# Part of a sparse expert layer moved from row gathers to dense products

## The chip, the cores and the metric

One core of a Trainium2 chip runs the whole program. The metric is the device time of one execution in microseconds. A core has a tensor engine (PE), a vector engine (VectorE, DVE), an activation engine (ScalarE, ACT), GpSimd (POOL) and a queue engine (SyncE, SP). Data come from HBM through 16 DMA engines. GpSimd issues the gathers, SP the plain loads, and both kinds share these engines.

## The reference

The program is one transformer layer on 256 latent tokens of width 2048: attention and a gated delta rule side by side, then an expert layer, then a final norm. The change touches the expert layer alone. Each token picks 16 of 16,384 experts for each of 8 heads, through two lists of 128 keys; an expert's number is `128 * i + j`, so there are 128 blocks of 128 experts. Each expert has one row of `u` and one row of `v`, 2048 floats each (8 KiB).

```python
q = (hx @ w_q).reshape(t, 8, 2, 128)
s = jnp.einsum('thpd,pkd->thpk', q, sub_keys)
top_s, top_i = lax.top_k(s, 16)
cand = top_s[:, :, 0, :, None] + top_s[:, :, 1, None, :]
cand_idx = top_i[:, :, 0, :, None] * 128 + top_i[:, :, 1, None, :]
best_s, best_pos = lax.top_k(cand.reshape(t, 8, -1), 16)
idx = jnp.take_along_axis(cand_idx.reshape(t, 8, -1), best_pos, axis=-1)
wts = jax.nn.softmax(best_s, axis=-1)
act = jax.nn.gelu(jnp.einsum('td,thkd->thk', hx, u[idx]), approximate=False)
return jnp.einsum('thk,thkd->td', wts * act, v[idx])
```

## The kernel before

The 256 tokens are two tiles `t` of 128, and the 8 heads two halves `f`. The layer ahead of the experts leaves its input in `hx`, channels on partitions. What follows has five stages.

Queries: for each head two tiles of `w_q` (1 MiB each, loaded by SP into row buffers) meet `hx` in 32 products of 256 columns (`query`), and two small products give the scores (`scores`). `route` turns the scores of a head and a token tile into 16 expert numbers and weights, wholly on VectorE, in small pieces (`piece`) between other work. The u rows of tile 0, half 0 are gathered meanwhile.

Rounds 0 to 2 (`rounds`, `n`): the round of tile and half `(t, f)` has 16 steps `b`. In each step `first` is called four times for the round after: it gathers 128 u rows, one per token (1 MiB), and VectorE multiplies them by the tokens' inputs `h_` and sums (a `SCALAR_TENSOR_TENSOR` of 128 x 2048). Then `second` gathers four times 128 v rows, and PE adds them up with weights in `zw`: 16 products of 32 weight columns by 512, four PSUM tiles `y`, four column groups of 32. `weigh`, at a round's start, applies gelu and the softmax weights and spreads the result into `zw`. Round 3 has v gathers alone.

Products and transposes of PE go through a helper at lines 192 and 197 and all work of DVE through one at line 181, so the profile gives these lines for them; gathers are line 1279. PE and DVE keep the order in which the program is written, and each engine waits in its own order: an instruction that waits holds what is queued behind it. The row buffers of `first`, `second` and the loads of `w_q` are one ring of 13 (`ROWS_R`, `ROWS_L`); an issue waits until the reader of its buffer is done. Besides, a gather's completion is signalled on one of eight semaphores in turn (`DMASW0` to `DMASW7`), and an issue waits for the gather eight before it.

`h_` is a PSUM tile of four banks that PE transposes fill (`hx_tokens`). `finish` adds the result of a token tile to `x1s` and applies the last norm, with two row buffers of its own; for tile 0 it runs in round 2.

Of the kernel before, what the change touches and what calls it, by code (L numbers as in the profile page):

```python
# [26 lines left out]
NEG = -1.0e30  # L27

# [83 lines left out]
def layout(x, c, ctx, c_ctx, w_mod, b_mod, norm1_w, w_in, mla_q_norm_w, mla_kv_norm_w, w_uq, w_ukv, dn_conv_w,  # L112
# [49 lines left out]
    a["u"] = np.ascontiguousarray(peer_u[0])  # L162
    a["v"] = np.ascontiguousarray(peer_v[0])
# [5 lines left out]
def tile_block(ctx: ExitStack, tc: tile.TileContext, I, out, dbg=None, upto=99):  # L169
# [1006 lines left out]
    hx = hxp.tile([128, KB, T], F32, name="hx")  # L1176
# [59 lines left out]
    ROWS_R, ROWS_L = 4, 9  # L1236
    rows = {"n": 0}

    def row():
        i = rows["n"] % (ROWS_R + ROWS_L)  # L1240
        rows["n"] += 1
        p, n = (rp, ROWS_R) if i < ROWS_R else (ex, ROWS_L)
        return p.tile([128, D], F32, name="row", bufs=n)

    def wq_load(i):
        r = row()
        sp.dma_start(r, I["wq"][i])
        return r

    ahead = [wq_load(i) for i in range(4)]  # L1250
# [11 lines left out]
    psa, st_psa = open_pool("psa", space=bass.MemoryType.PSUM)  # L1262
    psb, st_psb = open_pool("psb", space=bass.MemoryType.PSUM)

    def psm(tag):
        return psb.tile([128, 512], F32, name="ps_" + tag, tag=tag, bufs=2)

    def hx_tokens(t):

        o = psa.tile([128, D], F32, name="ps_h", tag="a", bufs=1)  # L1270
        for k in range(KB):
            pe.transpose(o[:, k * 128:(k + 1) * 128], hx[:, k, t * 128:(t + 1) * 128], ident)
        return o

    ex, st_ex = open_pool("ex", side=L)
# [7 lines left out]
    loaded = {"n": 8}  # L1283
    ahead += [wq_load(i) for i in range(4, 8)]
# [13 lines left out]
    for t in range(2):  # L1298
        per.append({n: ex.tile([128, 128], dt, name="%s%d" % (n, t)) for n, dt in
                    (("bs", F32), ("ef", F32), ("ix", U32), ("ixT", U32), ("a", F32))})  # L1300

    def scores(h, q, t, p):
# [3 lines left out]
        if t == 0 and h < 4:  # L1306
            s = ex.tile([128, T], F32, name="s", bufs=2)
        else:
            s = sc[:, h - 4 if t == 0 else 4 + h]
# [3 lines left out]
    def route(t, h, s):  # L1313
# [3 lines left out]
        sml = ex.tile([128, 208], F32, name="sml", bufs=2)  # L1317
# [6 lines left out]
        ij = sml[:, 176:208]  # L1324
# [33 lines left out]
        dve.tensor_reduce(ij, eq3, axis=AX.X, op=OP.add)  # L1358
        dve.scalar_tensor_tensor(ef[:, hs], ij[:, 0:16], 128.0, ij[:, 16:32], op0=OP.mult, op1=OP.add)
# [30 lines left out]
    def first(t, c, h_):  # L1390

        r = gather("u", per[t]["ix"][:, c:c + 1])
        dve.scalar_tensor_tensor(r, r, 1.0, h_, op0=OP.mult, op1=OP.mult, accum_out=per[t]["a"][:, c:c + 1])

    def weigh(t, f):
# [4 lines left out]
        dve.tensor_tensor(a, a, bs, op=OP.mult)  # L1400
        by_choice(lambda u, p, g: zw[f][p, g, 16 * u:16 * u + 496:33], a)

    def second(t, f, b, y):
# [3 lines left out]
        for c in range(4):  # L1407
            cs = slice(c * 512, (c + 1) * 512)
            for g in range(4):
                pe.matmul(y[c][32 * g:32 * g + 32, :], zw[f][:, g, 32 * b:32 * b + 32], rows[g][:, cs],  # L1410
                          start=f == 0 and b == 0, stop=f == 1 and b == 15)

    def finish(t, y):
# [5 lines left out]
        if t == 0:  # L1419
            for i, c in enumerate(cs):  # L1420
                dve.tensor_tensor(tmp[:, c], y[i], g2r[:, c], op=OP.mult)
            yield
        for i, c in enumerate(cs):
            if t == 1:
                dve.tensor_tensor(tmp[:, c], y[i], g2r[:, c], op=OP.mult)
            dve.tensor_tensor(x[:, c], x[:, c], tmp[:, c], op=OP.add)
# [21 lines left out]
    def piece():  # L1448

        while work:  # L1450
            if next(work[0], work) is not work:
                return
            work.pop(0)
# [8 lines left out]
    def query(h, parts):  # L1462

        ws = [ahead.pop(0) for _ in range(2)]
        os_ = [psm("mm") for _ in range(2)]
        q = [ex.tile([128, T], F32, name="q", bufs=4) for _ in range(2)]
        p = psm("g")
        for a, z in parts:
            for j in range(2):
                for k in range(KB):  # L1470
                    pe.matmul(os_[j][:, a:z], ws[j][:, k * 128:(k + 1) * 128], hx[:, k, a:z],
                              start=k == 0, stop=k == KB - 1)
                act.copy(q[j][:, a:z], os_[j][:, a:z])
# [12 lines left out]
    S = {}  # L1486
# [3 lines left out]
    for h in range(1, NH):  # L1490
        all_of(query(h, ((0, 256),)))
        if h < 5:
            work.append(route(0, h, S[h, 0]))
            for c in range(h * 16 - 16, h * 16):
                first(0, c, h_)
                if c % 16 > 2:
                    piece()
                if c % 8 == 7:
                    ahead.append(wq_load(loaded["n"]))
                    loaded["n"] += 1  # L1500
            while work:
                piece()
    for dst, src in ((g2r, modc[:, 80:96]), (fwr, cols[:, C_FN:C_FN + 16])):
        for i in range(0, 16, 4):
            p = psm("g")
            for j in range(4):
                pe.transpose(p[:, j * 128:(j + 1) * 128], src[:, i + j:i + j + 1].to_broadcast([128, 128]), ident)
            act.copy(dst[:, i * 128:(i + 4) * 128], p)
# [55 lines left out]
```

## Time and profile before

| what | value |
|---|---|
| time, median of 3 runs | 2511.69 us (2511.13 to 2518.51) |
| time of the profiled execution | 2511.01 us |
| its span | 2509.2 us |
| PE, DVE, ACT, POOL busy | 1766.9, 1582.4, 700.8, 897.6 us |
| mean DMA rate over the span | 318 GB/s |
| moved by gathers and other GpSimd DMAs | 541.44 MB |
| moved by SP's loads and stores | 246.39 MB |

Busy times of different engines overlap; their sum says nothing. The span is what the profiler saw, and the time is 1.8 us longer than it. Times inside the span count from its start.

### The profile page before, as it was taken

How to read it: one execution, taken by the hardware profiler on the slowest of the kernel's cores; microseconds unless marked ns; L12 is line 12 of the kernel's file. 1: busy time of each engine (PE TensorE's matmuls, PEld its weight loads, DVE VectorE, ACT ScalarE, POOL GpSimd, SP SyncE). 2: the span in 40 equal slices, each digit the busy share in tenths (PEclk: the TensorE clock that was granted, in tenths of full speed). 3: DMA queues.
4: the chain of work that ended last, by engine and by line, in shares of the span. 5: the costliest groups of instructions: out<-in, count | busy, mean ns of one | idle time of the engine just before them, and what ended most of it. 6: DMA issues, size and time to landing. Idle time of an engine off the chain costs nothing.

```text
span 2509.2 us, 28451 instructions
## 1 busy us (share of the span) xinstructions
PE 1766.9 (70%) x9988; PEld 1113.4 (44%) x9988; DVE 1582.4 (63%) x2773; ACT 700.8 (28%) x1636; POOL 897.6 (36%) x1108
## 2 busy tenths in 40 slices
PE   6999889988989999898953545454454544554665
PEld 2578778877878877898843100010000000000111
DVE  5358877778776588885899776656664454444001
ACT  4358556566655543354000100000000010000000
POOL 0000776738476000211333333333333333333331
PEclk8999999999999999999976776777666766667898
DMA  9955433555466587896999999999999989999997
GB/s 327 322 186 168 151 123 102 157 160 169 146 199 201 185 292 251 277 324 227 413 426 421 426 427 427 427 427 426 427 427 427 427 340 426 427 427 426 427 426 309
DMA packets 167375, 796.86 MB, mean 318 GB/s; under 512 B 26273, under 2 KB 45729, under 8 KB 99137
## 3 DMA queue, kind: packets, MB, share of 16 engines
q0 software_dynamic: 75296, 541.44, 51.5%
q1 hardware_dynamic: 76848, 246.39, 29.2%
q10 hardware_dynamic: 15088, 7.22, 1.0%
q8 instruction: 78, 1.28, 0.2%
q14 instruction: 65, 0.52, 0.1%
HBM read 784.75 MB, written 10.23 MB: 317 GB/s over the span
## 4 chain that ended last, share of the span: by engine, by line
DMA 53%; PE 20%; DVE 8%; issue 7%; POOL 6%; ACT 4%; SPq 0%; POOLq 0%; DVEq 0%; ACTq 0%
DMA row<-in_v,ixT 40%; PE ps_mm L192 13%; PE ps_d L192 4%; DMA row<-in_u,ix 4%; DMA raw<-in_wmod 3%; POOL qs L835 3%; POOL tq L833 3%; DMA raw<-in_wout 2%; DVE lo L181 2%; PE ps_r L192 2%; DMA mraw<-in_wmod 1%; DVE row L181 1%; POOL row L1279 1%; ACT hi L259 1%; PE ps_o L192 1%
## 5 line engine op out<-in xcount | busy, mean ns | idle before, releaser
L192 PE MATMUL ps_y<-row,zw 128*32 128x512 f32 x2048 | 573.3, 772 | 521.5 <-DMA row<-in_v,ixT 496.1
L181 DVE SCALAR_TENSOR_TENSOR row<-row,ps_h 128x2048 f32<-128x2048 f32 x256 | 582.1, 2281 | 409.5 <-DMA row<-in_u,ix 398.0
L192 PEld LDWEIGHTS ps_y<-row,zw 128*32 128x32 f32 x2048 | 97.8, 132 | 995.8 <-DMA row<-in_v,ixT 788.3
L1279 POOL DMA_INDIRECT row<-in_v,ixT x256 | 242.9, 949 | 405.4 <-DMA row<-in_v,ixT 302.9
L1279 POOL DMA_INDIRECT row<-in_u,ix x256 | 239.9, 937 | 408.3 <-DMA row<-in_u,ix 242.3
L181 DVE TENSOR_TENSOR lo<-raw,hi 128x512 fp32r<-128x512 f32 x408 | 307.3, 769 | 73.4 <-ACT hi L259 70.3
L192 PE MATMUL ps_mm<-h_hi,hi 128*128 128x256 f32 (+1 forms) x1040 | 341.0, 328 | 10.7 <-DVE gst L181 10.7
L192 PE MATMUL ps_mm<-h_hi,lo 128*128 128x256 f32 (+1 forms) x1040 | 323.4, 311 | 13.3 <-DVE lo L181 13.2
L192 PE MATMUL ps_mm<-h_lo,hi 128*128 128x256 f32 (+1 forms) x1040 | 322.9, 310 | 0.0
L259 ACT CAST hi<-raw 128x512 fp32r<-128x512 f32 x408 | 245.1, 619 | 184.7 <-PE ps_mm L192 123.0
L192 PEld LDWEIGHTS ps_mm<-h_hi,hi 128*128 128x128 f32 x1040 | 203.4, 196 | 31.3 <-DVE gst L181 11.7
L192 PEld LDWEIGHTS ps_mm<-h_hi,lo 128*128 128x128 f32 x1040 | 203.0, 195 | 24.0 <-DVE lo L181 14.5
L192 PEld LDWEIGHTS ps_mm<-h_lo,hi 128*128 128x128 f32 x1040 | 203.4, 196 | 9.3 <-issue 1.2
L835 POOL TENSOR_TENSOR qs<-qs,tq 32x30 f32<-32x30 f32 (+14 forms) x240 | 175.4, 731 | 18.7
L833 POOL TENSOR_TENSOR tq<-qs 32x30 f32<-32x30 f32 (+14 forms) x240 | 170.0, 708 | 18.1
L192 PE MATMUL ps_mm<-hx,row 128*128 128x256 f32 (+1 forms) x576 | 126.7, 384 | 49.6 <-DMA row<-in_wq 46.2
L192 PEld LDWEIGHTS ps_mm<-hx,row 128*128 128x128 f32 x576 | 108.4, 207 | 66.3 <-DMA row<-in_wq 47.9
L1399 ACT ACTIVATE a<-a 128x64 f32<-128x64 f32 x4 | 1.0, 256 | 464.6 <-DVE row L181 464.6
L1382 ACT ACTIVATE bs<-bs 128x64 f32<-128x64 f32 x4 | 1.0, 256 | 404.9 <-DVE bs L181 404.9
L181 DVE TENSOR_TENSOR row<-ps_y,g2r 128x512 f32<-128x512 f32 x8 | 5.2, 678 | 165.8 <-PE ps_y L192 165.8
L181 DVE SCALAR_TENSOR_TENSOR mraw<-mraw,crow 128x1024 f32<-128x1024 f32 x73 | 91.8, 1260 | 18.0 <-DMA mraw<-in_wmod 17.6
L181 DVE SCALAR_TENSOR_TENSOR raw<-raw,crow 128x1024 f32<-128x1024 f32 x55 | 71.9, 1307 | 44.9 <-DMA raw<-in_wmod 44.8
(367 smaller groups left out, 2819.8 us busy)
## 6 DMA issues: line engine op xcount, KB each, us to landing
raw<-in_win SPq DMA_DIRECT2D x130, 512.0 KB, 4.4
raw<-in_wmod SPq DMA_DIRECT2D x119, 512.0 KB, 4.9
mraw<-in_wmod SPq DMA_DIRECT2D x73, 512.0 KB, 4.9
raw<-in_wout SPq DMA_DIRECT2D x32, 512.0 KB, 5.4
row<-in_wq SPq DMA_DIRECT2D x16, 1024.0 KB, 9.2
raw<-in_wbb SPq DMA_DIRECT2D x16, 512.0 KB, 5.9
raw<-in_wba SPq DMA_DIRECT2D x16, 512.0 KB, 5.0
wraw<-in_win SPq DMA_DIRECT2D x48, 128.0 KB, 4.9
```

Of the source, the lines that this page charges most:

```text
L181: ins = f(*a, **k)
L192: ins = nc.tensor.matmul(*a, **k)
L259: act.copy(hi, raw)
L833: pool.tensor_tensor(t, m[:, 0:s, s:s + 1].to_broadcast([32, s, w]), m[:, s:s + 1, s + 1:32].to_broadcast([32, s, w]), op=OP.mult)
L835: pool.tensor_tensor(m[:, 0:s, s + 1:32], m[:, 0:s, s + 1:32], t, op=OP.add)
L1279: pool.indirect_dma_start(out=r, out_offset=None, in_=I[table], in_offset=bass.IndirectOffsetOnAxis(ap=ix, axis=0))
L1382: act.activation(bs, bs, AF.Exp)
L1399: act.activation(a, a, AF.Gelu)
```

## The change

The last 36 of the 128 blocks of experts (numbers from 11,776 on) leave the gathers. Their `u` blocks, transposed on the host, are multiplied with all 256 tokens (`dense_firsts`), gelu goes into `gd`; their weights are built as products of one-hot rows (`weights`), multiplied into `gd` (`merge`), and the result meets their `v` blocks (`dense_seconds`). A gather gets an index bound: a row above it is skipped, its buffer keeps what it held, and `weigh` sets its weight to zero.

SP loads the dense blocks and `w_q` in units of 512 KiB, through a ring of five (`UNITS`); a unit is loaded when PE is done with the one five before. The ring of row buffers has 7 (`ROWS`), all cleared at the start, and serves gathers and `finish` alone. `h_` lies in SBUF, and the u product writes to `junk`. `finish(0)` moves to round 3. The work is spread so: 24 of the 72 units of `dense_firsts` among the queries, 48 in round 0 (four and three a step, behind `second`), `weights` in round 1, 56 units of `dense_seconds` in round 2 and 16 in round 3 (two a step).

```diff
+NI, I0 = 36, 92
+E0 = I0 * 128
...
-    ROWS_R, ROWS_L = 4, 9
+    UNITS, ROWS = 5, 7
...
+    def load_unit():
+        if srcs:
+            u = rp.tile([128, 1024], F32, name="du", bufs=UNITS)
+            sp.dma_start(u, srcs.pop(0))
+            ahead.append(u)
...
         pool.indirect_dma_start(out=r, out_offset=None, in_=I[table],
-                                in_offset=bass.IndirectOffsetOnAxis(ap=ix, axis=0))
+                                in_offset=bass.IndirectOffsetOnAxis(ap=ix, axis=0),
+                                bounds_check=E0 - 1, oob_is_err=False)
...
+    for _ in range(ROWS):
+        pool.memset(row(), 0.0)
...
-        dve.scalar_tensor_tensor(r, r, 1.0, h_, op0=OP.mult, op1=OP.mult, accum_out=per[t]["a"][:, c:c + 1])
+        dve.scalar_tensor_tensor(junk, r, 1.0, h_, op0=OP.mult, op1=OP.mult, accum_out=per[t]["a"][:, c:c + 1])
...
+        dve.scalar_tensor_tensor(a, per[t]["ef"][:, fsl], float(E0), a, op0=OP.is_lt, op1=OP.mult)
...
+    def dense_first(o, i, hf):
+
+        w = ahead.pop(0)
+        for k in range(8):
+            pe.matmul(o[:, :T], w[:, k * 128:(k + 1) * 128], hx[:, hf * 8 + k], start=hf == 0 and k == 0,
+                      stop=hf == 1 and k == 7)
+        load_unit()
+        if hf == 1:
+            act.activation(gd[:, i], o[:, :T], AF.Gelu)
...
+            dve.tensor_tensor(oj, ijb[:, 1, g:g + 8][:, :, None].to_broadcast([128, 8, 128]),
+                              iota[:, None, :].to_broadcast([128, 8, 128]), op=OP.is_equal)
+            dve.tensor_tensor(oi, ijb[:, 0, g:g + 8][:, :, None].to_broadcast([128, 8, NI]),
+                              iota[:, None, I0:I0 + NI].to_broadcast([128, 8, NI]), op=OP.is_equal)
+            dve.tensor_tensor(oi, oi, ijb[:, 2, g:g + 8][:, :, None].to_broadcast([128, 8, NI]), op=OP.mult)
+            pw = psm("u")
+            for j in range(8):
+                pe.matmul(pw[:, j * NI:(j + 1) * NI], oj[:, j], oi[:, j], start=True, stop=True)
...
+                for t in range(2):
+                    for c in range(2):
+                        pe.matmul(e[c] if t == 0 else y[1][2 * hf + c], gd[:, i, t * 128:(t + 1) * 128],
+                                  w[:, c * 512:(c + 1) * 512], start=t == 0 and i == 0,
+                                  stop=t == 0 and i == NI - 1, skip_group_check=True)
...
+            if n == 0:
+                dense(df, 4 if b % 2 == 0 else 3)
+            if n == 2:
+                dense(ds, 4 if b % 2 == 0 else 3)
+            if n == 3:
+                dense(ds, 2)
```

GpSimd's queue, a step of round 0 before: four u gathers, then four v gathers, each with what it waits for (`PE` and `DVE` are the readers of the row buffer, `DMASW` an older gather).

```order
L1279 DMA row_14282<-in_u,ix0_13311 128x2048 [waits DMASW6_49,DVE_49]
L1279 DMA row_14288<-in_u,ix0_13311 128x2048 [waits DMASW7_49,PE_49]
L1279 DMA row_14294<-in_u,ix0_13311 128x2048 [waits DMASW0_49,PE_49]
L1279 DMA row_14299<-in_u,ix0_13311 128x2048 [waits DMASW1_49,PE_49]
L1279 DMA row_14305<-in_v,ixT0_13312 128x2048 [waits DMASW2_49,PE_49]
L1279 DMA row_14307<-in_v,ixT0_13312 128x2048 [waits DMASW3_49,DVE_49]
L1279 DMA row_14309<-in_v,ixT0_13312 128x2048 [waits DMASW4_49,DVE_49]
L1279 DMA row_14311<-in_v,ixT0_13312 128x2048 [waits DMASW5_49,DVE_49]
```

With 13 buffers the reader waited for stands 13 row buffers back, in the step before or the one before that. The same queue, the second step of round 0, with the change:

```order
L1295 DMA row_14698<-in_u,ix0_13318 128x2048 [waits DMASW7_49,DVE_49]
L1295 DMA row_14709<-in_u,ix0_13318 128x2048 [waits DMASW0_49,DVE_49]
L1295 DMA row_14721<-in_u,ix0_13318 128x2048 [waits DMASW1_49,DVE_49]
L1295 DMA row_14729<-in_u,ix0_13318 128x2048 [waits DMASW2_49,PE_49]
L1295 DMA row_14739<-in_v,ixT0_13319 128x2048 [waits DMASW3_49,PE_49]
L1295 DMA row_14743<-in_v,ixT0_13319 128x2048 [waits DMASW4_49,PE_49]
L1295 DMA row_14747<-in_v,ixT0_13319 128x2048 [waits DMASW5_49,PE_49]
L1295 DMA row_14751<-in_v,ixT0_13319 128x2048 [waits DMASW6_49,DVE_49]
```

The reader waited for now stands seven buffers back: the fourth u gather and the three v gathers after it take the buffers of the four v rows of the step before.

PE's queue in round 0 before, at the end of one step's `second` and the start of the next:

```order
L192 MATMUL ps_y3_14161<-row_14305,zw0_13303 32x512
L192 MATMUL ps_y3_14161<-row_14307,zw0_13303 32x512
L192 MATMUL ps_y3_14161<-row_14309,zw0_13303 32x512
L192 MATMUL ps_y3_14161<-row_14311,zw0_13303 32x512
L192 MATMUL ps_y0_14158<-row_14358,zw0_13303 32x512 [waits DMASW2_49]
```

The next step's `second` stood right behind. The same place with the change (`du` is a unit of a dense `u` block, `ps_u` its result):

```order
L196 MATMUL ps_y3_14562<-row_14751,zw0_13310 32x512
L196 MATMUL ps_u_14771<-hx_11192,du_14556 128x256 [waits DMAHW7_49,Activation_49]
L196 MATMUL ps_u_14771<-hx_11192,du_14556 128x256 x7
L196 MATMUL ps_u_14771<-hx_11192,du_14663 128x256 [waits DMAHW0_49]
L196 MATMUL ps_u_14771<-hx_11192,du_14663 128x256 x7
L196 MATMUL ps_u_14793<-hx_11192,du_14673 128x256 [waits DMAHW1_49,Activation_49]
L196 MATMUL ps_u_14793<-hx_11192,du_14673 128x256 x7
L196 MATMUL ps_y0_14559<-row_14847,zw0_13310 32x512 [waits DMASW2_49]
```

Three units of eight products now stand between one step's `second` and the next (four in every other step).

## Rows read from the trace of the kernel before

**Rows 1.** Page: GB/s in 40 equal slices; queue of GpSimd's DMAs (packets, MB, share).

```profile
GB/s 327 322 186 168 151 123 102 157 160 169 146 199 201 185 292 251 277 324 227 413 426 421 426 427 427 427 427 426 427 427 427 427 340 426 427 427 426 427 426 309
...
q0 software_dynamic: 75296, 541.44, 51.5%
```

**Rows 2.** Page: the chain that ended last, by line.

```profile
DMA row<-in_v,ixT 40%; PE ps_mm L192 13%; PE ps_d L192 4%; DMA row<-in_u,ix 4%; DMA raw<-in_wmod 3%; POOL qs L835 3%; POOL tq L833 3%; DMA raw<-in_wout 2%; DVE lo L181 2%; PE ps_r L192 2%; DMA mraw<-in_wmod 1%; DVE row L181 1%; POOL row L1279 1%; ACT hi L259 1%; PE ps_o L192 1%
```

**Rows 3.** Windows of the five stages, columns in the first row.

```profile
core 0: us, PE busy (x) PEld busy (x) DVE busy (x) ACT busy (x) POOL busy (x), PEclk, DMA share, GB/s
1192.00:1394.00 202.00, 124.38 (x529) 104.01 (x528) 188.62 (x296) 21.15 (x62) 73.09 (x78) 0.80 1.01 421
1394.00:1709.00 315.00, 159.10 (x532) 28.72 (x530) 203.62 (x380) 14.60 (x60) 120.82 (x127) 0.70 1.01 427
1709.00:2024.00 315.00, 157.17 (x514) 25.01 (x512) 179.18 (x260) 9.99 (x38) 120.58 (x128) 0.70 1.01 427
2024.00:2351.00 327.00, 164.25 (x546) 26.95 (x546) 145.01 (x140) 12.11 (x34) 120.51 (x129) 0.70 0.98 410
2351.00:2509.20 158.20, 95.93 (x476) 20.18 (x474) 10.42 (x22) 3.82 (x10) 46.84 (x50) 0.87 0.90 380
```

**Rows 4.** Waits from 1380 us on: who waited for whom, us, times, longest.

```profile
PE ps_y L192 <- DMA row<-in_v,ixT: 496.1, 222, 11.1
...
POOL row L1279 <- DMA row<-in_v,ixT: 302.9, 196, 4.1
```

**Rows 5.** Timeline, PE: the rest of two steps' `second` (start, length).

```profile
1513.31 3.62 PE L192 MATMUL ps_y<-row,zw 128*32 128x512 f32 x26 [0.51 <-DMA row<-in_v,ixT]
...
1532.88 5.51 PE L192 MATMUL ps_y<-row,zw 128*32 128x512 f32 x26 [0.56 <-DMA row<-in_v,ixT]
```

**Rows 6.** Timeline: the first gathers and the first products on their rows.

```profile
1190.77 1.02 POOL L1279 DMA_INDIRECT row<-in_u,ix  x1 [13.62 <-DVE ix L181]
1192.09 0.96 POOL L1279 DMA_INDIRECT row<-in_u,ix  x1 [0.30 <-issue]
...
1196.78 2.29 DVE L181 SCALAR_TENSOR_TENSOR row<-row,ps_h 128x2048 f32<-128x2048 f32 x1 [6.29 <-DMA row<-in_u,ix]
```

**Rows 7.** Timeline: the products of one head's query.

```profile
1189.90 13.98 PE L192 MATMUL ps_mm<-hx,row 128*128 128x256 f32 x64
```

**Rows 8.** Groups from 1400 us on: count, busy us, mean ns, idle before.

```profile
L181 DVE SCALAR_TENSOR_TENSOR row<-row,ps_h 128x2048 f32<-128x2048 f32 x187 | 426.6, 2282 | 395.4 <-DMA row<-in_u,ix 386.6 <-issue 4.6 <-DMA row<-in_v,ixT 0.6
...
L181 DVE TENSOR_TENSOR eq<-sml,iota 128x512 f32<-128x512 f32 x11 | 7.6, 693 | 0.4
...
L181 DVE TENSOR_TENSOR cf<-sml 128x256 f32<-128x256 f32 x10 | 4.2, 418 | 0.0
```

**Rows 9.** Timeline: a product of VectorE, and a gather's issue under it.

```profile
1528.45 0.69 DVE L181 TENSOR_TENSOR eq<-eq,sml 128x512 f32<-128x512 f32 x1
1528.65 1.30 POOL L1279 DMA_INDIRECT row<-in_v,ixT  x1 [1.51 <-DVE row L181]
...
1531.13 0.94 POOL L1279 DMA_INDIRECT row<-in_v,ixT  x1 [1.17 <-DMA row<-in_v,ixT]
```

**Rows 10.** Timeline, GpSimd: two issues near the start of round 2.

```profile
2044.67 0.94 POOL L1279 DMA_INDIRECT row<-in_v,ixT  x1 [17.82 <-ACT row L1427]
...
2055.80 0.94 POOL L1279 DMA_INDIRECT row<-in_u,ix  x1 [7.71 <-PE ps_y L192]
```

**Rows 11.** Timeline: the rest of the last step's `second`.

```profile
2491.65 3.62 PE L192 MATMUL ps_y<-row,zw 128*32 128x512 f32 x26 [1.35 <-DMA row<-in_v,ixT]
```

**Rows 12.** Timeline: the first step's `second`, in round 0.

```profile
1393.57 6.61 PE L192 MATMUL ps_y<-row,zw 128*32 128x512 f32 x32 [4.28 <-ACT zw L1372]
```

**Rows 13.** Groups of GpSimd before the first gather: a clearing of 128x2048.

```profile
L1294 POOL MEMSET zw<- 128x2048 f32 x2 | 3.6, 1811 | 22.7 <-ACT hx L1231 22.7
```

More of the change, by code (lines that the diff above doesn't have):

```diff
@@ new lines, in dense_firsts, with weights @@
+    def dense_firsts():
+        for i in range(NI):
+            o = psm("u")
+            for hf in range(2):
+                dense_first(o, i, hf)
+                yield
+    def weights(t):
+        p = psm("w")
+        ijb = ex.tile([128, 512], F32, name="eq", bufs=1)[:, :384].rearrange("p (a b) -> p a b", a=3)
+        for n, src in enumerate((per[t]["eij"][:, 0], per[t]["eij"][:, 1], per[t]["bs"])):
+            pe.transpose(p[:, n * 128:(n + 1) * 128], src, ident)
+        act.copy(ijb.rearrange("p a b -> p (a b)"), p[:, 0:384])
+        yield
+        last = None
+        for g in range(0, 128, 8):
+            z = g // 8 % 2
+            oj = hot[:, z * 1024:z * 1024 + 1024].rearrange("p (a b) -> p a b", a=8)
+            oi = hot[:, 2048 + z * 8 * NI:2048 + (z + 1) * 8 * NI].rearrange("p (a b) -> p a b", a=8)
+            dve.tensor_tensor(oj, ijb[:, 1, g:g + 8][:, :, None].to_broadcast([128, 8, 128]),
[6 more added lines that the diff above has]
+                pe.matmul(pw[:, j * NI:(j + 1) * NI], oj[:, j], oi[:, j], start=True, stop=True)
+            if last is not None:
+                merge(t, *last)
+            last = g, pw
+            yield
+        merge(t, *last)
+        yield
@@ L1413, in finish, with add_y @@
+    def add_y(t, c, p):
+        cs = slice(c * 512, (c + 1) * 512)
+        tmp = ex.tile([128, 512], F32, name="eq", bufs=1)
+        dve.tensor_tensor(tmp, p, g2r[:, cs], op=OP.mult)
+        dve.tensor_tensor(x1s[:, t, cs], x1s[:, t, cs], tmp, op=OP.add)
     def finish(t, y):
@@ L1462, in query @@
     def query(h, parts):
[L1464 to L1467, printed above, removed]
+        ws = [ahead.pop(0) for _ in range(4)]
+        os_ = [psm("y%d" % (2 * (h % 2) + j), 1) for j in range(2)]
+        q = [ex.tile([128, T], F32, name="q", bufs=2) for _ in range(2)]
+        p = psm("w")
         for a, z in parts:
@@ L1484, in first_queries, with dense @@
         return o
-    S = {}
+    def dense(g, n):
+        for _ in range(n):
+            next(g, None)
+    S, extra = {}, {}
     keep["on"] = True
@@ L1509, in tile_block @@
-    st_psb.close()
-    psy, st_psy = open_pool("psy", space=bass.MemoryType.PSUM)
-    def y_tile():
-        return [psy.tile([128, 512], F32, name="ps_y%d" % c, tag="y%d" % c, bufs=1) for c in range(4)]
+    all_of(query(1, ((0, 256),)))
+    df = dense_firsts()
+    for n, heads in enumerate(((2,), (3,), (4, 5), (6, 7))):
+        for h in heads:
+            all_of(query(h, ((0, 256),)))
+        work.append(route(0, n + 1, S[n + 1, 0]))
+        for c in range(n * 16, n * 16 + 16):
+            first(0, c, h_)
+            if c % 16 > 2:
+                piece()
+        while work:
+            piece()
+        dense(df, 8 if n < 2 else 4)
@@ L1527, in tile_block @@
                     first(t1, c, h_)
-                    piece()
+                    piece(2 if n == 0 and c % 2 else 1)
+            else:
+                piece()
             if b == 0:
@@ L1531, in tile_block @@
                 if n == 2:
-                    work.append(finish(0, y[0]))
-                    piece()
+                    for c in range(4):
+                        add_y(0, c, y[0][c])
                     y[1] = y_tile()
```

155 lines of the change are left out of this document (88 added, 67 removed).

## The prediction

> **What bounds the kernel now.** I read the strip of 40 slices first. From the 20th slice on, that is from about 1190 us, the DMA moves 413 to 427 GB/s almost without a break, and the queue of GpSimd's gathers carries 541 MB [rows 1]. The chain that ended last says the same: 40% of the span is the v gathers [rows 2]. Then I cut the end of the kernel into its five stages [rows 3]: the queries with the first u gathers (1192 to 1394), three rounds with u and v gathers (315, 315 and 327 us) and a last round with v gathers alone. The DMA share is 0.98 to 1.01 in the first four, PE is busy only about half of each round, and the granted clock is 0.70, between TensorE's two levels of 1.2 and 2.4 GHz.
>
> One step of a round is four u gathers, four v gathers, and the 16 products of `second`. The last v row of a step lands at 1513.31 and that of the next at 1532.88 [rows 5]: 19.6 us for eight gathers, 2.45 us each, which is 1 MiB at 427 GB/s. Both sides wait for the DMA: PE 496 us for v rows, GpSimd 303 us for an older gather to land before it issues the next [rows 4]. So there are always about eight gathers in the rings, and the time of a round is its bytes.
>
> **What the change takes off and adds in bytes.** I put the reference's inputs through its own routing and counted: 72.6% of the 32,768 choices lie below expert 11,776 (71.0, 73.1, 72.7 and 73.8% in the four rounds). If a skipped row moves nothing, 512 gathers lose 27.4% of 537 MB, 147 MB. The dense blocks add 36 x 2 MiB = 75.5 MB. The net 71 MB would be 167 us at 427 GB/s. That is the most the change could give, and it holds only if the rings stay full. A gather then costs between 1.79 us (its kept share) and 2.46 us (if every engine had a slice without a skipped row). I take 2.0, nearer to the kept share because several gathers queue and their gaps partly even out. A dense unit of 512 KiB costs 1.23 us.
>
> The Trainium skill ("DMA: Bandwidth & Descriptors", section The descriptor swizzle) says that each of the 16 engines writes eight fixed partitions of such a transfer. Counted so, the fullest engine has about 34 of its 40 rows in five gathers, 2.1 us each, and the sum below would be some 20 us longer. No row here shows it.
>
> **The ring of row buffers.** This is the part on which the forecast rests. Before, 13 buffers served eight gathers in flight. Now there are 7, and a step needs eight. In GpSimd's new order the fourth u gather of a step, and the first three v gathers behind it, wait for PE, because they reuse the buffers of the step before's v rows. `second` reads each row in all four of its column groups, so all four v rows come free only at its end. Call A the landing of a step's last v row and B the end of its `second`. B is A + 3.6 us when PE is at 2.4 GHz, 5.5 us when it is partly at 1.2 [rows 5]; I take 3.6, since the dense products keep PE busy just before. At A the rings hold only three u gathers, 3 x 1.79 = 5.4 us. The first gather that fills an idle ring landed 6.0 us after its issue began, of which 2.46 is transfer [rows 6]: 3.5 us of issue, start and completion. So after A the data of the next gather starts at 3.6 + 3.5 = 7.1 us, 1.7 us after the rings ran dry, and then five gathers have to pass before the next A.
>
> The price of one step is therefore: 3.6 (`second`) + 3.5 (refill) + 5 x 2.0 (gathers) + 3 x 1.23 (the units that PE frees meanwhile, one every 3.5 us) = **20.8 us** with dense units, and 17.1 us without. Before it was 19.6. The trace of before shows one such stop: the buffers were out, GpSimd stood 17.8 us and then 7.7 us more for PE [rows 10], and that round took 327 instead of 315 us [rows 3]. The bounds: with kept bytes alone and no gap, 8 x 1.79 + 3.5 x 1.23 = 18.6; with 2.46 per gather and 5.5 us for `second`, 25.
>
> **PE.** A query tile's 64 instructions of 256 columns took 13.98 us, 0.218 each [rows 7]. A unit of `dense_first` is 16 of them, 3.5 us; a unit of `dense_seconds` is 8 of twice the columns, 3.5 us too. Per step that is 3.5 x 3.5 + 3.6 = 15.9 us, inside 20.8, so PE does not bind rounds 0 and 2.
>
> **DVE and GpSimd.** The token-by-row product takes 2.28 us [rows 8], and now it reads both inputs from SBUF. The trace shows what a two-input instruction of VectorE does to a gather's issue: an elementwise product of 0.69 us began at 1528.45, and the issue that started at 1528.65 took 1.30 us where others take 0.94 [rows 9]; it went on when the product ended. An issue that starts under the 2.28 us product can thus be held by up to 2.1 us. Three of them stand in a step after A. Most of that hides behind five transfers, since five issues of 1.24 us [rows 6] plus three holds are 12.5 us against 13.7 of transfers. I add 0.5 us to a round-0 step, where routing lengthens DVE's row of work, and 0.7 to a step without units, nothing elsewhere; the bounds are 0 and 2.1.
>
> The Trainium skill ("SBUF — State Buffer", section Who interferes with whom) states it as a rule: a VectorE instruction with two SBUF inputs contends with a GpSimd instruction that reads SBUF. By that rule, and the trace agrees, this hold is new in every u gather.
>
> In round 1 the one-hot weights join: 32 groups, each with a comparison of 1024 elements, one of 288, a product and a merge of 288. From 0.69 us for 512 and 0.42 for 256 [rows 8], that is 1.2 + 3 x 0.46 = 2.6 us. With 2.36 us for a u row and its accumulator, a piece each on four rows of a step is 19.9 us for DVE. It binds the first nine steps (36 pieces); seven more go at 17.1 + 0.7.
>
> **Stage by stage** (all times those of the profiled execution, whose own time is 2511.0 us, 0.7 under the median of the runs).
> - Queries: `second` first ended at 1393.57 + 6.61 = 1400 [rows 12]. 24 units of dense work go to PE here, 84 us on top of 124 of 202 [rows 3]: 208, so PE ends 6 us late. Seven clearings of row buffers at 1.81 us [rows 13] fit into GpSimd's idle 13.6 us ahead of the first gather [rows 6]. First B: 1406.
> - Round 0: 48 units last 13.7 steps: 13.7 x 21.3 + 2.3 x 17.8 = 333.
> - Round 1: 9 x 19.9 + 7 x 17.8 = 304.
> - Round 2: 56 units, 16 steps x 20.8 = 333.
> - Round 3, to the last B: eight steps with two units, PE-bound, 3.6 + 2 x 3.5 = 10.6; seven without, 3.5 + 2.0 + 3.6 = 9.1; and 12 us for `finish(0)`, which now takes two of the seven buffers here, the price it had in round 2 before [rows 3]: 85 + 64 + 12 = 161.
> - Tail: the last `second` ended at 2495.3 [rows 11], 14 us before the span's end; it stays.
>
> 1406 + 333 + 304 + 333 + 161 + 14 = 2551, plus the 1.8 us that lie around the span: **2553 us, 1.7% slower**. The bytes fall, but the rings no longer stay full, and what is saved per gather is paid back as refill.
>
> **The rivals.**
> - *The rings stay full* (faster). If the three u gathers in flight last until the next data, that is if 7.1 us shrinks to 5.4 or unit loads fill the gap, each stage goes by its bytes: round 0 is 16 x 14.3 + 48 x 1.23 = 288, round 1 is 9 x 19.9 + 7 x 14.3 = 279, round 2 is 229 + 69 = 298, round 3 is 85 + 7 x 7.2 + 12 = 147. With 1406, 14 and 2 that is 2434. For it: loads and gathers ran together at 421 GB/s in the stage of the queries [rows 3]. Against it: the waits for PE in GpSimd's new order. The point of decision is a step of about 20.0 us in rounds 0 and 2; below it the change pays. Chance 0.27.
> - *Skipped rows save nothing*, because the engines still handle them. Then a step is 19.6 + 4.3 = 24 with units: 13.7 x 24 + 2.3 x 19.6 = 374, 16 x 19.9 = 318, 384, and 8 x 12.3 + 7 x 9.8 + 12 = 179; with 1410 and 16, about 2680. Nothing in the trace speaks for or against it. Chance 0.05.
> - *PE turns into the bound* because the clock stays at the lower level: a unit is then 7 us and a step 5.5 + 3.5 x 7 = 30. For it: 0.70 granted in these rounds now. Against: 0.80 where PE had the query products [rows 3], and PE will be busy three quarters of a step, not half. If a quarter of the steps of rounds 0 and 2 went so, 30 x 0.25 x 9.2 = 69 us more: 2620. Chance 0.06.
>
> **How the numbers follow.** My forecast has 0.62; its own range is 2500 to 2605, which is 1 us a step either way over 48 steps. Faster by over 0.3% takes the first rival's 0.27 and 0.04 from the low end of my own case, where a step comes out under 20: 0.31. Within 0.3%, about 7.5 us and about what a measurement of this kernel can tell from no change: 0.06. Slower: 0.63. The range of 2440 to 2620 leaves out the lowest of the first rival and the skip that saves nothing.
>
> **What would show it.** In the changed profile GpSimd's gathers should wait for PE in every step of rounds 0 and 2, the DMA share of those rounds should fall to some 0.9, last landings of a step should lie 20 to 22 us apart, and gather issues should show up to 3 us where a u product runs. The prediction is wrong if the DMA share stays at 1.0 with steps near 18.5 (then the refill is hidden), or if the software queue still moves 540 MB (then nothing is skipped).

## The result, and the profile after

The changed kernel takes 2743.93 us (median of 4 runs, 2734.05 to 2754.26) against 2511.41 for the kernel before (4 runs): a ratio of 1.092, interval 1.087 to 1.097. It is 9% slower, where 1.7% was forecast, and lies above the range. The profiled execution took 2754.26 us.

The page of the changed kernel, first the strip and GpSimd's queue, as in [rows 1], then the two groups of gathers (mean ns of one issue behind the comma):

```profile
GB/s 319 318 159 177 125 119 144 161 157 146 206 198 201 271 270 303 245 280 370 385 314 300 297 329 344 322 259 270 247 289 277 304 332 300 323 313 299 356 310 209
...
q0 software_dynamic: 75296, 394.60, 38.7%
...
L1295 POOL DMA_INDIRECT row<-in_u,ix x256 | 382.8, 1495 | 574.0 <-PE ps_y L196 429.0
L1295 POOL DMA_INDIRECT row<-in_v,ixT x256 | 397.4, 1552 | 185.9 <-PE ps_y L196 88.5
```

The bytes did fall, from 541 to 395 MB, but the rate fell with them, from 427 to some 300 GB/s. An issue now takes 1.5 us on average where an undisturbed one takes 0.94 [rows 9]. The same five stages as in [rows 3]:

```profile
core 0: us, PE busy (x) PEld busy (x) DVE busy (x) ACT busy (x) POOL busy (x), PEclk, DMA share, GB/s
1175.00:1426.00 251.00, 212.19 (x1042) 182.03 (x1042) 215.55 (x350) 30.17 (x87) 152.88 (x85) 0.93 0.89 341
1426.00:1818.00 392.00, 319.54 (x1383) 187.26 (x1382) 245.87 (x511) 37.97 (x111) 194.84 (x129) 0.86 0.83 312
1818.00:2172.50 354.50, 214.08 (x979) 106.68 (x978) 222.34 (x249) 4.21 (x18) 205.63 (x129) 0.67 0.78 277
2172.50:2569.00 396.50, 330.65 (x962) 108.84 (x962) 138.39 (x125) 5.21 (x19) 185.65 (x124) 0.88 0.82 313
2569.00:2752.50 183.50, 139.72 (x608) 42.98 (x607) 17.88 (x40) 7.55 (x20) 56.91 (x57) 0.86 0.78 285
```

No engine is full in rounds 0 to 2: the DMA share is 0.78 to 0.83, PE is busy 0.60 to 0.83 of the time, VectorE 0.35 to 0.63. Work that waits in a circle looks like this. Against the forecast: the first B (end of a step's `second`) came at 1426 (1406), round 0 took 392 us (333), round 1 355 (304), round 2 396 (333), round 3 to the last B 170 (161).

One step at the end of round 0 shows the circle. PE, GpSimd and VectorE in the timeline (start, length, idle before):

```profile
1708.46 1.05 PE L196 MATMUL ps_y<-row,zw 128*32 128x512 f32 x2
1709.77 1.05 PE L196 MATMUL ps_y<-row,zw 128*32 128x512 f32 x2 [0.26 <-DMA row<-in_v,ixT]
1713.52 1.92 PE L196 MATMUL ps_y<-row,zw 128*32 128x512 f32 x2 [2.71 <-DMA row<-in_v,ixT]
1716.30 5.36 PE L196 MATMUL ps_y<-row,zw 128*32 128x512 f32 x26 [0.86 <-DMA row<-in_v,ixT]
...
1721.09 0.99 POOL L1295 DMA_INDIRECT row<-in_u,ix  x1 [8.63 <-PE ps_y L196]
1722.39 1.01 POOL L1295 DMA_INDIRECT row<-in_v,ixT  x1 [0.30 <-issue]
1723.70 1.90 POOL L1295 DMA_INDIRECT row<-in_v,ixT  x1 [0.30 <-issue]
1725.90 0.99 POOL L1295 DMA_INDIRECT row<-in_v,ixT  x1 [0.31 <-issue]
1727.19 2.94 POOL L1295 DMA_INDIRECT row<-in_v,ixT  x1 [0.30 <-DVE sml L185]
...
1726.99 2.27 DVE L185 SCALAR_TENSOR_TENSOR junk<-row,ht 128x2048 bf16<-128x2048 f32 x1
```

Three things are to be seen. GpSimd stood 8.6 us until `second` was all but done (it ended at 1721.66), as foretold. Its last issue began 0.2 us after a u product of VectorE and took 2.94 us: the product ended at 1729.26, and 0.87 us later the issue was done. And PE had no more dense work at 1708.5; it waited for v rows in pieces, its clock fell (the same two instructions took 1.05 us, then 1.92), and the rest of `second` took 5.36 us where [rows 5] has 3.62 at its shortest. The granted clock is in the column before the last two, for three stretches of this step and for the two rows of [rows 5] in the kernel before:

```profile
1697.00:1708.00 11.00, 11.00 (x53) 8.97 (x49) 10.79 (x26) 0.39 (x1) 9.38 (x5) 1.00 0.81 280
1708.40:1716.30 7.90, 4.07 (x8) 0.46 (x7) 1.61 (x6) 0.38 (x1) 3.14 (x4) 0.79 1.00 396
1716.30:1721.70 5.40, 5.40 (x27) 1.31 (x28) 3.04 (x7) 0.00 (x0) 0.61 (x1) 0.67 0.74 310
...
1513.00:1517.00 4.00, 3.62 (x26) 0.90 (x26) 1.27 (x1) 0.00 (x0) 1.47 (x2) 1.00 1.01 426
1532.80:1538.40 5.60, 5.51 (x26) 1.21 (x26) 3.01 (x6) 0.00 (x0) 1.87 (x2) 0.65 1.01 424
```

The same 26 instructions take 3.62 us at 1.00 and 5.4 to 5.5 at 0.65 to 0.67.

### The profile page after: what moved, and what is told of

Its sections match the earlier page's. It is cut to its first block, busy times and chain, and to the rows that moved or that the text cites. A ratio compares the mean times of both kernels' runs of the same rounds, so it can differ in the third digit from the quotient of the medians.

```text
span 2752.5 us, 33962 instructions
## 1 busy us (share of the span) xinstructions
PE 2269.4 (82%) x12234; PEld 1522.7 (55%) x12234; DVE 1688.7 (61%) x2913; ACT 724.7 (26%) x1684; POOL 1205.5 (44%) x1115
## 3 DMA queue, kind: packets, MB, share of 16 engines
q0 software_dynamic: 75296, 394.60, 38.7%
## 4 chain that ended last, share of the span: by engine, by line
DMA 26%; issue 22%; PE 20%; DVE 16%; POOL 11%; ACT 3%; POOLq 0%; SPq 0%; DVEq 0%; ACTq 0%
PE ps_mm L196 11%; DMA row<-in_u,ix 10%; POOL row L1295 6%; DVE junk L185 6%; DMA row<-in_v,ixT 6%; DMA raw<-in_wmod 3%; PE ps_d L196 3%; PE ps_y L196 3%; POOL qs L839 2%; POOL tq L837 2%; DMA raw<-in_wout 2%; DMA mraw<-in_wmod 2%; PE ps_r L196 2%; DVE lo L185 2%; DVE hx L185 1%
## 5 line engine op out<-in xcount | busy, mean ns | idle before, releaser
L185 DVE SCALAR_TENSOR_TENSOR junk<-row,ht 128x2048 bf16<-128x2048 f32 x256 | 585.5, 2287 | 513.0 <-DMA row<-in_u,ix 510.2
L196 PE MATMUL ps_y<-row,zw 128*32 128x512 f32 x2048 | 487.1, 806 | 278.0 <-DMA row<-in_v,ixT 235.8
L1295 POOL DMA_INDIRECT row<-in_u,ix x256 | 382.8, 1495 | 574.0 <-PE ps_y L196 429.0
L1295 POOL DMA_INDIRECT row<-in_v,ixT x256 | 397.4, 1552 | 185.9 <-PE ps_y L196 88.5
L196 PE MATMUL ps_u<-hx,du 128*128 128x256 f32 x1152 | 253.0, 380 | 0.0
L196 PEld LDWEIGHTS ps_u<-hx,du 128*128 128x128 f32 x1152 | 217.4, 190 | 41.2 <-issue 12.3
L196 PE MATMUL ps_u<-hx 128*128 128x36 f32 x512 | 97.3, 364 | 52.9 <-DVE hx L185 52.7
L196 PE MATMUL ps_y<-du,gd 128*128 128x512 f32 x288 | 135.3, 592 | 0.0
L196 PEld LDWEIGHTS ps_u<-hx 128*128 128x128 f32 x512 | 93.9, 283 | 62.4 <-issue 54.3
L196 PE MATMUL ps_y<-hx,du 128*128 128x256 f32 (+1 forms) x576 | 116.8, 366 | 3.5 <-ACT hx L1235 3.5
```

The lines of the kernel that those rows point to most:

```text
L185: ins = f(*a, **k)
L196: ins = nc.tensor.matmul(*a, **k)
```

## The experiments

Each ran on one chip beside the kernel before, whose median was 2506 to 2514 us; ratios are to that kernel's runs, with their interval. Differences in us between runs of different batches carry some 6 us of that spread. "A step" is the mean spacing of the last v issue of a step within a round, from the timeline: in the changed kernel 1409.9 to 1776.8 over 15 spacings, 24.5 us in round 0, then 22.8, 25.3 and 11.7.

**Hold, and ring.** The u product with one SBUF input:

```diff
-        dve.scalar_tensor_tensor(junk, r, 1.0, h_, ..., accum_out=per[t]["a"][:, c:c + 1])
+        dve.tensor_reduce(per[t]["a"][:, c:c + 1], r, axis=AX.X, op=OP.add)
```

> The u product becomes a sum over the gathered row alone (one SBUF input in place of two, same length); the tokens' inputs are left out of it. Hold theory: gather issues no longer stop under VectorE's product, so their mean falls from 1.50 to about 0.95 us, the query stage loses the 20 us it was over the forecast, and rounds 0 to 2 lose 1 to 2 us a step: 2640 to 2680 us. Ring theory (what costs is that the gathers of the next step wait for the end of `second`): the issues get short, but the steps lose under 0.5 us; 2705 to 2730. Clock theory (`second` at TensorE's lower level is the loss): within 10 us of 2744.

2649.89 us, 1.058 (1.055 to 1.061), in the range of the hold theory. VectorE's instruction is as long as before (2278 ns), and the issues are short:

```profile
L185 DVE TENSOR_REDUCE a<-row 128x1 f32<-128x2048 f32 x256 | 578.2, 2278 | 422.5 <-DMA row<-in_u,ix 421.8
...
L1295 POOL DMA_INDIRECT row<-in_u,ix x256 | 263.6, 1030 | 723.0 <-PE ps_y L196 472.1
...
L1295 POOL DMA_INDIRECT row<-in_v,ixT x256 | 259.4, 1013 | 195.3 <-PE ps_y L196 87.5
```

Steps: 22.6, 20.9, 22.9, 11.7. The hold is worth 94 us (86 by the ratios), 1.8 to 2.4 a step; the query stage gave back 5 us of the 20 expected. This instruction also writes no row, but the kernel before settles that point: its u product wrote whole rows, with one input in SBUF and one in PSUM, and its gather issues took 0.94 us:

```profile
L1279 POOL DMA_INDIRECT row<-in_u,ix x256 | 239.9, 937 | 408.3 <-DMA row<-in_u,ix 242.3
```

So it is the second SBUF input that holds an issue.

The Trainium skill ("SBUF — State Buffer", section Who interferes with whom, as in the prediction) says that a VectorE instruction with at most one SBUF input, outside VectorE's two-port modes, does not contend with GpSimd. The trace agrees, with issues of 1.03 and 1.01 us.

`second` in pairs of rows:

```diff
-        for c in range(4):
-            for g in range(4):
+        for c, g in [(c, g) for q in ((0, 1), (2, 3)) for c in range(4) for g in q]:
```

> `second` goes through rows 0 and 1 first, in all four column groups, then rows 2 and 3. The first two buffers come free before the last row has landed. Ring theory: two more gathers are under way when the last row lands, so the refill hides, and a step with dense units falls from 24.6 to 20 to 22 us, one of round 1 from 22.2 to 20; with round 3 about 2590 to 2650 us. Hold theory: the issues are held as before; at most 1 us a step, 2700 to 2744. Against both: pairs use half of the array's column groups, so if the first pair cannot run early, `second` doubles from 5.4 to some 9 us and the step gets 2 to 4 us longer: 2840 to 2930.

2592.74 us, 1.036 (1.034 to 1.037), in the range of the ring theory. Steps: 21.1, 20.9, 20.8, 11.4. The first pair now runs before the last row lands, and two issues go out ahead of the end:

```profile
1527.65 4.19 PE L196 MATMUL ps_y<-row,zw 128*32 128x512 f32 x16 [0.85 <-DMA row<-in_v,ixT]
1534.20 5.32 PE L196 MATMUL ps_y<-row,zw 128*32 128x512 f32 x14 [2.36 <-DMA row<-in_v,ixT]
...
1530.70 0.99 POOL L1295 DMA_INDIRECT row<-in_u,ix  x1 [1.47 <-PE ps_y L196]
1531.99 0.99 POOL L1295 DMA_INDIRECT row<-in_v,ixT  x1 [0.30 <-issue]
1538.66 0.99 POOL L1295 DMA_INDIRECT row<-in_v,ixT  x1 [5.68 <-PE ps_y L196]
```

The holds are as before (issues of 1.40 and 1.62 us), and yet 151 us are gone (142 by the ratios): the order in which buffers come free costs by itself.

Then two kernels without dense work (its generators return at once; the second gathers every row, bound 16383):

> All dense work and the loads of its units are left out, and so are the 27% of the choices that they serve; the gathers still skip their rows. Ring theory: a step is `second` 5.4, refill 3.5 to 5, five gathers at 2.0: 19 to 20 us in rounds 0 to 2, 11 in round 3; with the first end of `second` at 1400 about 2500 to 2560 us. Skip theory (a skipped row costs an engine as much as a kept one): steps of 21.5 or more, over 2600. If the rings stayed full the steps would be 14.3: 2300.

2594.62 us, 1.035 (1.033 to 1.037); steps 20.8, 21.3, 21.2, 10.7. The time lies between the two theories' ranges. The ring theory's figure plus the hold would be 5.4 + 3.5 + 5 x 2.0 + 1.9 = 20.8, but `second`, from its first product on the last row to its end, took only 4.4, 4.9 and 5.0 us here, so about 1 us of a step lies in terms that no run parts. From here to the changed kernel are 3.6 us in round 0 (three units a step at 1.23 make 3.7) and 4.0 in round 2 (3.5 units, 4.3). So the units cost at most what was forecast; part of the difference is the longer `second`.

> The work of the kernel before (all rows gathered, no dense part) with the changed buffers: ring of seven, tokens' inputs in SBUF, units of 512 KiB. Ring theory: a step cannot fall below its bytes, 19.6 us, and has 5.4 + 3.5 to 5 + 5 x 2.45 = 21 to 22.7: 2560 to 2620 us. Hold theory: the same holds as in the changed kernel, some 2 us a step: 2600 to 2650, with issues of 1.5 us. If neither the ring nor the hold costs anything: 2511, as before.

2690.74 us, 1.074 (1.072 to 1.077), above both figures: the same work as before, with seven buffers and `h_` in SBUF, is 185 us slower, at 22.4 to 22.9 a step. The change of buffers, without any dense work, loses four fifths of what the whole change loses.

**Do the two causes add?**

> Pairs in `second`, and the u product as a sum over the gathered row alone (the tokens' inputs left out): both edits at once. Alone they took 94 and 151 us off. Two separate causes (hold and ring): the gains add up to some 200 to 245 us, 2500 to 2545 us, steps of 18.5 to 19.5 us. One cause seen twice (the pairs give the held issues the time that they lose): no better than 2570.

2558.47 us, 1.019 (1.017 to 1.022): 185 us off, where 94 and 151 make 245 (by the ratios 183, where 86 and 142 make 228). Neither expectation holds as stated; the causes are distinct but overlap, since an issue that is held costs only while the rings are about to run dry.

> All rows gathered, no dense part, the changed buffers, and the u product as a sum over the row alone (tokens' inputs left out). With the two-input product this was 2691 us at 22.4 to 22.9 us a step. Hold theory: without it 20 to 21 us a step, 2590 to 2630. If the ring of seven alone keeps the loss: above 2660. If the hold was all of it: 19.6 us a step and 2520 to 2550.

2613.60 us, 1.041 (1.036 to 1.046), in the range of the hold theory; steps 21.6, 21.2, 20.9. Of the 185 us of the run with all rows gathered, 77 are the hold; the other 108 stay with the ring of seven and whatever else of the changed kernel that run keeps.

The other way about, the hold with a long ring (the kernel before):

```diff
-    ROWS_R, ROWS_L = 4, 9
+    ROWS_R, ROWS_L = 4, 8
...
+        ht = ex.tile([128, D], F32, name="ht", bufs=1)
+        for i in range(0, D, 512):
+            act.copy(ht[:, i:i + 512], o[:, i:i + 512])
```

> The kernel before with the tokens' inputs in SBUF, and 12 row buffers in place of 13: the hold without the short ring. If the hold costs only where the rings run dry: issues of 1.5 us, but eight of them are 12 us inside 19.6 of transfers, so 2505 to 2530. If it costs by itself, some 2 us a step as in the changed kernel: 2580 to 2620.

2506.56 us, 0.9995 (0.9978 to 1.0012). The page's strip and the gathers:

```profile
GB/s 337 323 180 173 152 135 94 166 160 180 145 196 191 200 289 272 273 322 209 421 417 412 422 426 427 426 427 426 427 427 427 427 387 426 427 426 427 427 426 307
...
L1282 POOL DMA_INDIRECT row<-in_u,ix x256 | 502.5, 1963 | 233.5 <-PE ps_y L192 90.7
L1282 POOL DMA_INDIRECT row<-in_v,ixT x256 | 266.7, 1042 | 290.3 <-DMA row<-in_v,ixT 185.7
```

A u gather's issue takes 1.96 us, more than in the changed kernel, and the eight issues of a step 12.0 us, as many as there (12.2). Yet they cost nothing: 427 GB/s as before. The hold has no price of its own; it gets one where too few transfers are queued to cover it.

The hold made shorter, with the full product (and pairs):

```diff
-        dve.scalar_tensor_tensor(junk, r, 1.0, h_, ...)
+        for q in range(4):
+            qs = slice(q * 512, (q + 1) * 512)
+            dve.scalar_tensor_tensor(r[:, qs], r[:, qs], 1.0, h_[:, qs], op0=OP.mult, op1=OP.mult,
+                                     accum_out=per[t]["a4"][:, q, c:c + 1])
```

> Pairs in `second`, and the u product cut into four instructions of 512 elements, with the tokens' inputs (nothing left out). If an issue is held only until the running instruction ends, the hold shrinks from up to 2.1 us to up to 0.6: issues of 1.1 to 1.2 us, 2520 to 2570 us. If the issue waits through all four, as through one long one: issues of 1.5 us and 2590 to 2620, a little slower than the pairs alone because VectorE's product gets some 0.2 us longer.

2578.87 us, 1.027 (1.024 to 1.030), 14 less than pairs alone, with issues of 1.09 and 1.06 us. The issue is let in between instructions, so cutting a long one is a cure that keeps the result. The time lies between the two figures: of the 34 us that the hold still cost with pairs (2592.74 less 2558.47), the quarters got 14, with VectorE's four instructions busy for 2.52 us where one took 2.29.

**Round 1.** In the run with pairs and one input the spacings of round 1 were 20.6 to 25.2 us from the second to the eighth, and 15.0 to 17.6 in the second half, where the one-hot work is done. The one-hot products stand in PE's queue ahead of `second` and wait for VectorE, which multiplies the u row whose buffer the last `second` freed. That run's PE in round 1:

```profile
1814.52 1.98 PE L196 MATMUL ps_u<-hx 128*128 128x36 f32 x16
...
1823.80 3.60 PE L196 MATMUL ps_u<-hx 128*128 128x36 f32 x16 [6.95 <-DVE hx L185]
1827.33 7.86 PE L196 MATMUL ps_y<-row,zw 128*32 128x512 f32 x32
```

So `weights` was spread over the round (on top of pairs and quarters):

```diff
-                    piece(2 if n == 0 and c % 2 else 1)
+                    if n != 1 or c % 4 < 2:
+                        piece(2 if n == 0 and c % 2 else 1)
```

> As the run with pairs and quarters, but `weights` goes two pieces a step through all of round 1 instead of four a step through its first half, and round 3 has `second` in one go again; nothing is left out. Loop theory (in round 1 the one-hot products stand ahead of `second` on PE and wait for VectorE, which waits for the u row whose buffer `second` frees): all steps of round 1 at 16 to 18 us, the round falls from 320 to 270 and the time from 2579 to 2515 to 2540. If VectorE's amount of work is the bound, spreading it changes nothing: 2565 to 2590.

2564.34 us, 1.021 (1.019 to 1.023), between the two figures. Round 1 fell to 18.6 a step from 20.6, not to 17, and round 3, in one go again, gave some of it back (11.8 from 11.4). The order matters, for about 2 us a step.

**The clock.** A filler of products behind the dense units of round 0:

```diff
+                o = psm("u")
+                for k in range(20):
+                    pe.matmul(o[:, :T], ident, subk.rearrange("p a b -> p (a b)"), start=True, stop=True)
```

> 20 products of 256 columns, whose result nobody reads, stand behind the dense units of each step of round 0, so PE idles less ahead of `second`. Clock theory: `second` falls from 5.6 to about 4.2 us, the granted clock of round 0 from 0.86 to 0.95 or more, and a step of round 0 by 1 to 1.5 us: 2720 to 2730. If the clock is not what lengthens the step, round 0 keeps its 24.5 us or gets longer by what the filler delays: 2744 to 2780.

2757.45 us, 1.097 (1.093 to 1.100), not clearly different from the changed kernel; round 0 at 25.1. `second` did fall to 3.64 us, at a granted clock of 0.98 from 1412 to 1787, but the filler was two instructions a product and too long:

```profile
1476.77 14.08 PE L196 MATMUL ps_u<-hx,du 128*128 128x256 f32 x64
1490.68 8.80 PE L196 MATMUL ps_u<-subk,ck 128*128 128x256 f32 x40
1499.41 3.64 PE L196 MATMUL ps_y<-row,zw 128*32 128x512 f32 x32
```

14.1 + 8.8 + 3.6 is 26.5 us, so PE became the bound in steps with four units. The run shows that PE at 2.4 GHz has the 3.6 us of the forecast; what the step would gain from that alone stays open.

**The skipped rows.**

> No dense work, and the bound at expert 0, so nearly every row is skipped; the expert layer's sums are left out. It measures the price of a skipped row. Skip theory, from the changed profile (0.11 us of an engine for each): 65,536 packets over 16 engines are 450 us of GpSimd's queue, 19 to 21% of a span of some 2200 us; the queue's packet count stays at 75,296. If a skipped row costs nothing, the queue's share is about 1%. If it costs as a kept one, about 50%.

2239.86 us in one execution, and the queue:

```profile
q0 software_dynamic: 75296, 4.84, 2.1%
```

The packets are all there, but they take 47 us of each engine in all (2.1% of 2237.8), about 0.01 us for one. The skip theory's 19 to 21% falls. Among kept rows, in a ring that never runs dry (`bounds_check=16383 if rows["n"] < 48 else 11775` in the kernel before):

> The kernel before with the index bound alone: ring of 13, no dense part; the choices of the last 36 blocks are left out (their rows keep old contents). It prices a skipped row among kept ones, in a ring that never runs dry. If it costs next to nothing there too (the run with all rows skipped: 2.1% of the span for 65,536 packets, 0.01 us each): a step of eight gathers 14.3 us, the three rounds 229 us each, 2220 to 2260 us. If a skipped row among kept ones costs 0.1 us, as the changed profile's queue share suggests: 16.2 us a step, 2310 to 2350.

2261.57 us, 0.900 (0.896 to 0.904), just above the cheap range; 14.9, 15.2 and 16.2 us a step.

```profile
GB/s 340 313 221 169 154 134 127 119 153 159 163 146 190 194 208 225 282 265 293 323 241 377 417 350 300 421 409 411 401 411 381 416 409 289 392 413 409 414 407 278
...
q0 software_dynamic: 75296, 405.08, 44.5%
```

A gather costs 1.9 us (15.2 / 8); the forecast had 2.0. The packets' time, 44.5% of 2253.3 us, is 36 us over what 405 MB take at the rate of [rows 1] (1292 us for 541 MB), 0.03 us for each of 16,645 skipped rows. Why the changed kernel's share suggests 0.11 is seen in the run with all rows gathered and seven buffers: no row skipped, and still 51.2% of 2690.5, 1378 us for the same 541 MB. Packets last longer where the rings are interrupted; the share of a queue is not its work.

**The length of the ring.** All with pairs, quarters and spread `weights`, and fewer dense blocks where buffers need the room:

```diff
-    UNITS, ROWS = 5, 7
+    UNITS, ROWS = 4, 8
...
-NI, I0 = 36, 92
+NI, I0 = 32, 96
```

> As the run before, with 32 blocks in dense products instead of 36, four units instead of five, and eight row buffers instead of seven; nothing is left out. If the ring still costs after the pairs, some 10 to 30 us less than the run before. If the DMA is full there already (a skipped row is a packet that costs about 0.1 us), within 12 us of it.

> 32 blocks in dense products, four units, but seven row buffers: it parts the two edits that took 56 us off. If the eighth buffer did it: 2550 to 2575, as with 36 blocks and seven buffers. If the smaller dense share did it: 2505 to 2525.

> As the run with 32 blocks and ring of eight, with 24 blocks in dense products and nine row buffers; nothing is left out. Ring theory: steps of rounds 0 and 2 fall further, below 19.6 us, and the time to 2460 to 2495, under the kernel before. If the ring is long enough at eight, the smaller dense share leaves more bytes to gather and the time is 2500 to 2530.

> The same with 16 blocks and ten row buffers; nothing is left out. Ring theory: the rings are full, and bytes alone count again: 2470 to 2500. If the ring is long enough at eight: 2510 to 2540.

| blocks, buffers | time (us) | ratio | steps of rounds 0 to 3 (us) |
|---|---|---|---|
| 32, 7 | 2568.08 | 1.022 (1.018 to 1.026) | 20.2, 18.8, 20.4, 11.4 |
| 32, 8 | 2508.35 | 1.000 (0.998 to 1.002) | 19.9, 17.9, 20.6, 10.5 |
| 24, 9 | 2483.50 | 0.988 (0.984 to 0.991) | 19.2, 17.2, 20.8, 9.0 |
| 16, 10 | 2496.38 | 0.993 (0.991 to 0.995) | 18.9, 18.2, 20.6, 9.2 |

The eighth buffer gave 60 us (54 by the ratios), more than the 10 to 30 expected, and the four blocks nothing (2564 with 36). With 24 blocks and nine buffers the kernel is 1.2% faster than the kernel before. Its rounds 0 to 2:

```profile
1415.00:1720.00 305.00, 222.35 (x923) 107.10 (x924) 262.91 (x930) 25.86 (x89) 133.01 (x128) 0.86 0.98 396
1720.00:1996.00 276.00, 208.69 (x1016) 113.38 (x1014) 223.39 (x622) 9.26 (x27) 147.81 (x128) 0.72 0.97 390
1996.00:2317.00 321.00, 284.94 (x908) 105.59 (x909) 178.20 (x540) 7.78 (x26) 133.75 (x125) 0.94 0.98 397
```

The rings are nearly full again, at 390 to 397 GB/s. Steps of round 2 did not get shorter with the ring (20.4 to 20.8), against the expectation. With ten buffers the three rounds move 402 to 411 GB/s, but 16 blocks leave more rows to gather, and the time is 13 us longer than with nine.

Last, the ring alone, in the changed kernel without the three other edits (its u product written back to the row, which makes the room):

> The changed kernel with 36 blocks as they were and eight row buffers, four units, the u product written back to its row; nothing is left out. Ring theory: one buffer more lets one more gather be under way at the end of `second`, about 2 us a step in rounds 0 to 2: 2630 to 2670 us. If fewer units in the ring cost as much as a buffer gains: 2720 to 2760.

> The changed kernel with nine row buffers, 24 blocks in dense products, four units, and the u product written back to its row; no pairs, no quarters, no new order of `weights`; nothing is left out. Ring theory: with nine buffers the next step's gathers need not wait for the end of `second`, and the holds hide as they did with 12 buffers: 2500 to 2550 us. If the short ring was not the root, and the three edits of the order each cured a cost of its own: above 2600.

2608.64 us, 1.040 (1.035 to 1.045), with eight buffers: 135 us for one buffer, steps of 21.6, 21.5 and 21.6, more of a gain than expected. 2527.88 us, 1.006 (1.005 to 1.008), with nine and 24 blocks, in the range of the ring theory, its issues still 1.61 and 1.51 us. What the smaller dense share gave in this second run was not tested alone. An estimate: at seven buffers the kernel with 36 blocks takes 2743.93 us and the one with none 2690.74, 53 us for 36 blocks, so some 18 of the 216 us for 12. Nor was the place where the u product is written tested alone.

The three other edits together are worth 180 us with seven buffers (2743.93 to 2564.34), some 100 with eight (2608.64 to 2508.35, the latter with 32 blocks) and 44 with nine (2527.88 to 2483.50). So the length of the ring is the main cause, and the holds and the order of `second` are how a short ring is felt: the longer the ring, the less they cost, though at nine buffers they still cost something.

## Why the prediction was wrong

The direction, and the mechanism ("`second` reads each row in all four of its column groups, so all four v rows come free only at its end"), were right: GpSimd waits for PE in each step, and with nine row buffers (and 24 blocks) the loss is nearly gone. The price of a step is built as it was forecast, from `second`, refill, five gathers and units. Two of its terms failed, `second` and the hold, by about as much each; round 1 follows from them for the most part. Of the 200 us that the profiled execution lies above the forecast, rounds 0 to 2 have 173, at 59, 51 and 63.

- **`second`, a failed step.** "I take 3.6, since the dense products keep PE busy just before." They do not: in the step shown they end 7.8 us ahead of the rest of `second`, PE waits in pieces, and the granted clock falls from 1.00 to 0.67. From the first product on the last row to the end of `second` the traces have 5.2 us on average in round 0 and 5.5 in round 2 (4.5 in round 1, where the rows of the first eight steps had landed before). That is 1.6 and 1.9 us a step more than forecast, some 56 us over rounds 0 and 2. The bound of 5.5 was stated from [rows 5], and the wrong end taken: 3.6 is nearly the smallest value in the kernel before, whose mean in these rounds is 4.5 to 4.6.
- **The hold, the other failed step.** 0.5 us in round 0 and nothing in round 2, "most of that hides behind five transfers". Measured, by leaving it out: 1.8 and 2.4. An issue that is held delays all that stand behind it in GpSimd's queue, and with seven buffers the transfers in flight are too few to hide that; with 12 they hid all of it. With the measured `second` and hold, round 0 comes to 20.8 + 1.6 + 1.8 = 24.2 (measured 24.5) and round 2 to 20.8 + 1.9 + 2.4 = 25.1 (25.3). The sums close a little too well: `second` was 0.4 to 0.5 us shorter in the run without the hold, so that much is counted twice, and some 0.7 us a step stays open.
- **Round 1.** "It binds the first nine steps" with VectorE's 19.9 us. VectorE was never full (0.63 of the round). The steps took 22.8 where 19.9 and 17.8 were priced, 19.0 on average. The run without dense work has no one-hot products and still 21.3 a step, so 2.3 of the missing 3.8 us are there without it, and 1.5 are the one-hot work, in the loop over u row, one-hot products and `second`.

Right were the bytes of a gather (2.0 forecast, 1.9 measured with 13 buffers), the units (at most 3.6 and 4.0 a step), the low price of a skip, and round 3 within 9 us. The first B was 20 us late; 6 of it lie ahead of the first gather (1197.2 instead of 1190.8), and the rest is not settled: the run without holds gained 5 there from first gather to first v issue.

Of the rivals, full rings did not come about with seven buffers; with 13 and rows skipped they are real (15 us a step). PE as the bound came true only for the lower clock in `second`, not for the units.

## What to carry to other kernels

A ring of buffers that is shorter than one step's transfers turns everything that delays an issue or a release into time: count, at the moment the last transfer lands, how many are still queued, and price every term of the loop at its slow end when the answer is fewer than the loop needs. When a change takes memory from a ring, cost the ring first: here the eighth buffer was worth 60 to 135 us, and four dense blocks, at seven buffers, nothing. A share of engine or queue time is no price of an item; a run with nothing but that item is.

## What the runs showed of the hardware

- A gather's issue that starts under a VectorE instruction with two SBUF inputs ends about 0.9 us after that instruction; four instructions of 0.69 us let it in between (1.09 us mean), one of 2.28 us doesn't (1.40). Under a product of the same length with one input in SBUF and one in PSUM the issues took 0.94 us.
- A row skipped by the index bound keeps its packet (75,296 in the queue with and without) and costs 0.01 us alone and 0.03 among kept rows.
- `second` took 3.64 us for 32 instructions in a round with a granted clock of 0.98, and 5.36 for its last 26, at 0.67, after three stops of 0.3 to 2.7 us, though PE had worked without a break for the 11 us before them, at 1.00.
